# A decoder step in float32: inputs and outputs laid out by feature ahead of the launch, no turning of them on TensorE, products of ones while the first loads arrive

## The chip, the cores and the metric

The kernel runs on one core of a Trainium2 chip. The core has five engines that run beside each other: TensorE (PE in the rows; its weight loads are PEld), VectorE (DVE), ScalarE (ACT), GpSimd (POOL) and SyncE (SP), which here issues transfers. SBUF is the memory the engines work on, with 128 partitions; PSUM is what TensorE adds into; DRAM is reached by 16 DMA engines. The metric is device time in microseconds (us), lower is better. Before: 2800.08 us, median of three runs (2798.88 to 2800.47).

## The reference

One layer of a hybrid recurrent decoder for 272 prompt tokens (16 meta tokens, then 256) and eight sequences of eight sample tokens, together 336 columns; D = 2048, the feed-forward width is 5632.

```python
def layer(h, st, p, lead):
    s5_re, s5_im, C0, n0, m0, buf = st
    h = h + 0.5 * swiglu(rmsnorm(h, p['ffn1_norm']), p['ffn1_w_gate'], p['ffn1_w_up'], p['ffn1_w_down'])
    u = rmsnorm(h, p['mix_norm'])
    z = u @ p['w_in']
    y_s5, ns_re, ns_im = s5_mixer(z[..., :o0], ...)      # complex diagonal state space, GELU, gated linear unit
    y_ml, nC, nn_, nm, nbuf = mlstm_mixer(z[..., o0:o1], ...)   # causal convolution, matrix memory C, four heads
    gates = jax.nn.sigmoid(z[..., o5:])
    merged = gates[..., :D_MODEL] * (y_s5 @ p['w_branch_s5']) + gates[..., D_MODEL:] * (y_ml @ p['w_branch_mlstm'])
    h = h + merged @ p['w_out']
    h = h + 0.5 * swiglu(rmsnorm(h, p['ffn2_norm']), p['ffn2_w_gate'], p['ffn2_w_up'], p['ffn2_w_down'])
    return h, (ns_re, ns_im, nC, nn_, nm, nbuf)
# in a chunk of the mLSTM: num gets inter * einsum('nhvk,nlhk->nlhv', C0, q),
# and C = decay * C0 + einsum('nhs,nshv,nshk->nhvk', w_end, v, k)
```

After the layer the outputs are y = rmsnorm(h, final_norm) for the 256 + 64 = 320 live tokens, and the new states of S5, the mLSTM and the convolution.

## The kernel before

Activations lie by feature: a tile has 128 features on the partitions and the tokens as columns, 16 tiles for D. A large product takes a weight tile of 128 by 128 as the stationary operand and 336 columns (320 once the meta tokens are no longer needed) as the moving one. Every float32 number is split into two float32r parts, so a weight tile makes three products (`product`, L388 to L390: high by high, high by low, low by high).

`Weights` holds the order in which TensorE takes the weights. A load is 1 MB, a ring of three buffers (`wraw`) takes them from SyncE's queue, a load is issued when both halves of the load three before it have been split. A load has two halves of 24 products (four k tiles, two column tiles, three products each). `take` hands a half out and first emits the split of the half two ahead: ScalarE casts the high part (L95, tile `whi`), VectorE subtracts it (L96, `wlo`). All engines take their instructions in the order written; that order comes from the Python code, where generators (`tick`) put the small work of the mixers between the halves, one step a half, or two for those in `fast`.

At the start x lies in DRAM by token. `constants` loads it in three column pieces with halves of the first two weight loads between them; seven gain vectors come as rows over GpSimd's queue. `x_features` turns four tiles at a time on TensorE (L367 to L370, four pieces a tile), splits them (`norm_split`, L329 and L330) and copies them from PSUM to `h` (L377). The first pair of gate and up products (tile `sm`) runs between these groups: gate 0, turn, up 0, gate 1, turn, and so on, eight halves in all.

In the mixers TensorE also turns S5's parameters and states (L577, L583), S5's C matrices (L741), the convolution's old and new rows (L923, L924, L1117), the C state of the sample sequences before it is used (L1225, eight a value half, four heads by two value halves), the last S5 states (L1395) and the normaliser (L1294). A prompt's new memory is three products per value half (L1242).

In the last down product each finished pair of tiles is scaled by the final gain and turned back by token (`turned`, L1464), six turns a pair; `finish` sums squares over the partitions (L1477), takes the root (L1481), and ScalarE and VectorE scale the rows while the stores go out.

## Time and profile before

| what | us |
|---|---|
| three timed runs | 2800.47, 2800.08, 2798.88 |
| span of the profiled execution (first to last instruction) | 2797.4 |
| TensorE busy | 2776.8 |
| VectorE busy | 1600.3 |
| ScalarE busy | 1106.0 |
| GpSimd busy | 194.5 |

The profiled execution's own time is not given beside its span; the median of the timed runs is 2.7 us above it. Matmuls are pipelined and one's end is modelled, so a row's duration of 0.31 us holds the overlap with the next; the distance from start to start is what one costs. The DMA engines moved 459.03 MB, 164 GB/s over the span.

### The profile page before, as it was taken

The page shows a single profiled execution, that of the slowest core. Times are in us where ns is not written, and L with a number is a line of the kernel's source. Part 1 is how long each engine was busy: PE and PEld are TensorE (multiplying, and loading weights), DVE is VectorE, ACT ScalarE, POOL GpSimd, SP SyncE. Part 2 cuts the span into 40 slices and gives each one's busy share as a digit, 9 for nine tenths or more (in the row PEclk, how much of TensorE's full clock was granted, in tenths as well). Part 3 has the DMA queues.
Part 4 walks back from the last instruction along what each step waited for, and adds up shares of the span by engine and source line. Part 5 has one row for each costly group of instructions (what it writes and reads, how often), then busy time and mean ns, then how long its engine had stood idle before and what let it go on. Part 6 is the DMA issues. An engine that isn't in the chain of part 4 may idle for free.

```text
span 2797.4 us, 44767 instructions
## 1 busy us (share of the span) xinstructions
PE 2776.8 (99%) x18640; PEld 2759.9 (99%) x18640; DVE 1600.3 (57%) x2485; ACT 1106.0 (40%) x1617; POOL 194.5 (7%) x298
## 2 busy tenths in 40 slices
PE   9999999999999999999999999999999999999998
PEld 8999999999999999999999999999999999999998
DVE  6666565555544575767655556445445555445455
ACT  5433444444432353434344444443333333333334
POOL 4000001000000042000010100100000000000001
PEclk9999999999999999999999999999999999999999
DMA  6445544554444457566655666544444444454542
GB/s 183 148 137 179 156 160 159 186 166 158 157 165 141 140 178 197 188 197 203 205 166 170 204 200 206 172 148 151 151 152 150 151 151 147 142 164 137 165 146 88
DMA packets 375884, 459.03 MB, mean 164 GB/s; under 512 B 16338, under 2 KB 319422, under 8 KB 374641
## 3 DMA queue, kind: packets, MB, share of 16 engines
q1 hardware_dynamic: 360880, 417.33, 46.8%
q0 software_dynamic: 10336, 32.74, 3.4%
q10 hardware_dynamic: 4464, 6.09, 0.6%
q8 instruction: 147, 2.41, 0.4%
q14 instruction: 57, 0.46, 0.0%
HBM read 419.54 MB, written 36.57 MB: 163 GB/s over the span
## 4 chain that ended last, share of the span: by engine, by line
PE 97%; DVE 1%; ACT 1%; DMA 1%; issue 0%; SPq 0%; ACTq 0%; DVEq 0%
PE mm L388 30%; PE mm L390 30%; PE mm L389 30%; PE sm L388 1%; PE sm L390 1%; PE sm L389 1%; PE sm L1339 1%; PE sm L1232 0%; DVE slotB L330 0%; DVE wlo L96 0%; DMA aux<-u_dr 0%; PE sm L1384 0%; PE sm L765 0%; PE sm L1385 0%; PE sm L1225 0%
## 5 line engine op out<-in xcount | busy, mean ns | idle before, releaser
L96 DVE TENSOR_TENSOR wlo<-wraw,whi 128x1024 fp32r<-128x1024 f32 x727 | 881.9, 1225 | 653.5 <-ACT whi L95 652.8
L95 ACT CAST whi<-wraw 128x1024 fp32r<-128x1024 f32 x727 | 748.7, 1047 | 799.3 <-PE mm L389 774.3
L388 PE MATMUL mm<-slotA,whi 128*128 128x336 f32 (+1 forms) x2688 | 851.2, 317 | 0.3 <-DVE slotE L457 0.3
L390 PE MATMUL mm<-slotA,wlo 128*128 128x336 f32 (+1 forms) x2688 | 844.2, 314 | 0.0
L389 PE MATMUL mm<-slotB,whi 128*128 128x336 f32 (+1 forms) x2496 | 783.9, 314 | 0.0
L389 PE MATMUL mm<-quarter,whi 128*128 128x320 f32 (+1 forms) x1792 | 558.9, 312 | 0.0
L388 PEld LDWEIGHTS mm<-slotA,whi 128*128 128x128 f32 x2688 | 505.6, 188 | 2.8 <-issue 1.2
L390 PEld LDWEIGHTS mm<-slotA,wlo 128*128 128x128 f32 x2688 | 504.8, 188 | 0.2 <-DVE wlo L96 0.2
L388 PE MATMUL mm<-quarter,whi 128*128 128x320 f32 (+1 forms) x1536 | 481.2, 313 | 0.6 <-DVE slotE L457 0.6
L390 PE MATMUL mm<-quarter,wlo 128*128 128x320 f32 (+1 forms) x1536 | 480.4, 313 | 0.4 <-DVE wlo L96 0.4
L389 PEld LDWEIGHTS mm<-slotB,whi 128*128 128x128 f32 x2496 | 469.7, 188 | 1.2
L388 PE MATMUL mm<-slotB,whi 128*128 128x320 f32 x1472 | 455.1, 309 | 0.0
L390 PE MATMUL mm<-slotB,wlo 128*128 128x320 f32 x1472 | 454.8, 309 | 0.0
L389 PE MATMUL mm<-slotD,whi 128*128 128x320 f32 x1344 | 415.3, 309 | 0.0
L389 PEld LDWEIGHTS mm<-quarter,whi 128*128 128x128 f32 x1792 | 336.8, 188 | 0.0
L388 PEld LDWEIGHTS mm<-quarter,whi 128*128 128x128 f32 x1536 | 288.7, 188 | 1.1 <-issue 1.1
L390 PEld LDWEIGHTS mm<-quarter,wlo 128*128 128x128 f32 x1536 | 288.3, 188 | 0.8 <-DVE wlo L96 0.8
L388 PEld LDWEIGHTS mm<-slotB,whi 128*128 128x128 f32 x1472 | 276.3, 188 | 0.1
L390 PEld LDWEIGHTS mm<-slotB,wlo 128*128 128x128 f32 x1472 | 276.3, 188 | 0.0
L457 DVE SCALAR_TENSOR_TENSOR slotE<-mm,slotE 128x336 f32<-128x336 f32 (+1 forms) x352 | 171.4, 497 | 157.6 <-PE mm L390 148.7
L389 PEld LDWEIGHTS mm<-slotD,whi 128*128 128x128 f32 x1344 | 252.3, 188 | 0.1
L339 POOL TENSOR_TENSOR acc<-acc,sq 128x336 f32<-128x336 f32 (+1 forms) x58 | 61.1, 1054 | 1408.1 <-ACT sq L338 1406.1
(393 smaller groups left out, 1744.3 us busy)
## 6 DMA issues: line engine op xcount, KB each, us to landing
wraw<-in_ffn_w_down_dram SPq DMA_DIRECT2D x88, 1024.0 KB, 5.1
wraw<-in_ffn_w_gate_dram SPq DMA_DIRECT2D x87, 1024.0 KB, 5.1
wraw<-in_ffn_w_up_dram SPq DMA_DIRECT2D x87, 1024.0 KB, 5.1
wraw<-in_w_in_dram SPq DMA_DIRECT2D x64, 1024.0 KB, 5.7
wraw<-in_w_out_dram SPq DMA_DIRECT2D x16, 1024.0 KB, 5.5
w_dr<-slotD POOLq DMA_DIRECT2D x8, 1280.0 KB, 8.0
wraw<-in_w_branch_mlstm_dram SPq DMA_DIRECT2D x8, 1024.0 KB, 5.7
wraw<-in_w_branch_s_dram SPq DMA_DIRECT2D x8, 1024.0 KB, 5.5
```

What stands on the lines that cost most here:

```text
L95: k.nc.scalar.copy(hi, src)
L96: k.nc.vector.tensor_tensor(lo, src, hi.bitcast(F32), op=ALU.subtract)
L339: nc.gpsimd.tensor_tensor(self.acc[:, 0:n], self.acc[:, 0:n], sq, op=ALU.add)
L388: nc.tensor.matmul(ps[m], hi[:, k, c], a, start=first and k == 0, stop=False)
L389: nc.tensor.matmul(ps[m], hi[:, k, c], b, start=False, stop=False)
L390: nc.tensor.matmul(ps[m], lo[:, k, c], a, start=False, stop=last and k == 3)
L457: nc.vector.scalar_tensor_tensor(hm, ps[m], 0.5, hm, op0=ALU.mult, op1=ALU.add)
L1339: pe.matmul(ps[:, NSL * t:NSL * t + NSL], w1[:, a, t], u4[g % 2][:, t], start=True, stop=True)
```

## The change

A function outside the kernel (`lay_out`) writes the inputs in the layout that the tiles have: x by feature, with meta, prompt and sample tokens in one array; all vectors as columns of one array; the C state with the key on the partitions; every 1 MB weight load as one contiguous block of 128 rows of 8 KB. `lay_back` does the same for the outputs. No arithmetic is moved there except a repeated log_dt. In the kernel the turns of these are gone, each group of small loads is one load. The C state and its update keep the key on the partitions, so in the update v is now masked and split in place of k. The output is scaled by feature: the reciprocal root of the mean square is spread over partitions by three products, and 16 tiles are scaled, five on GpSimd, eleven on VectorE. At the start TensorE multiplies ones (`rouse`).

```diff
     def constants(self):
-        nc.scalar.dma_start(gain1, i["ffn1_norm"][0].rearrange("(a p) -> a p", p=P))
-        nc.scalar.dma_start(self.xs[2][64:80], meta)
-        for c, (lo, hi) in enumerate(((0, 512), (512, 1024), (1024, 2048))):
-            s = slice(lo, hi)
-            nc.sync.dma_start(self.xs[0][:, s], xp[0:128, s])
-            nc.sync.dma_start(self.xs[1][:, s], xp[128:256, s])
-            nc.sync.dma_start(self.xs[2][0:64, s], sm[:, s])
-            if c < 2:
-                self.w.load_half(0, c)
-                self.w.load_half(1, c)
+        xpart = lambda q, lo, hi: q.dma_start(e[:, NT * lo:NT * hi], i["x"][:, NT * lo:NT * hi])
+        nc.scalar.dma_start(cols[:, 0:120], i["vec"])
+        part(0, 0, 2)
+        xpart(nc.scalar, 0, 2)
+        xpart(nc.sync, 2, 4)
+        part(0, 2, 4)
+        part(1, 0, 4)
+        xpart(nc.sync, 4, 8)
+        part(0, 4, 8)
+        part(1, 4, 8)
+        xpart(nc.sync, 8, 12)
+        xpart(nc.sync, 12, 16)
...
+    def rouse(self):
+        pe = self.nc.tensor
+        o = self.ones
+        ps = self.mm_psum()
+        for _ in range(4):
+            pe.matmul(ps[:, 0:P], o, o, start=True, stop=True)
+        tiles = [self.mm_psum() for _ in range(3)]
+        for _ in range(5):
+            for t in (0, 1):
+                for m in (0, 1):
+                    pe.matmul(tiles[t][64 * m:64 * m + 64, 0:96], o[64 * t:64 * t + 64, 64 * m:64 * m + 64], o[64 * t:64 * t + 64, 0:96], start=True, stop=True)
+        for _ in range(4):
+            pe.matmul(tiles[2][:, 0:P], o, o, start=True, stop=True)
...
     def ffn(self, which):
-                        turned = self.x_features(0)
                         for part in range(2):
-                            next(turned)
                             self.w.first(part)
-                        next(turned, None)
+                            for m in (2 * part, 2 * part + 1):
+                                self.norm_split(m, h[:, m])
...
                             if which == 1 and ps is pg and j < 3:
-                                for _ in self.x_features(j + 1):
-                                    pass
+                                for m in range(4 * j + 4, 4 * j + 8):
+                                    self.norm_split(m, h[:, m])
...
     def mlstm(self):
-                for b in range(2):
-                    ps = self.sm_psum()
-                    for n in range(4):
-                        pe.transpose(ps[:, P * n:P * n + P], c0[b][:, n], self.ident)
-                    s.copy(c0t[b], ps)
-                yield from rest(2)
...
-                        pe.matmul(num[:, 256 + 8 * n:264 + 8 * n], c0t[n // 4][:, P * (n % 4):P * (n % 4) + P],
+                        pe.matmul(num[:, 256 + 8 * n:264 + 8 * n], c0[n // 4][:, n % 4],
...
-                up = self.sm_psum()
-                for t, n in enumerate((128, 112, 32)):
-                    pe.matmul(up[:, 0:P], vv(t, n), kw[0:n, t], start=t == 0, stop=t == 2)
+                if x == 0:
+                    up = self.sm_psum()
+                    for t, n in enumerate((128, 112, 32)):
+                        pe.matmul(up[:, 0:256], kw[0:n, t], self.vt[h][0:n, t], start=t == 0, stop=t == 2)
...
     def finish(self):
+        rb = self.sm_psum()
+        for t, (at, w) in enumerate(self.ENDS):
+            nc.tensor.matmul(rb[:, at:at + w], r[0:w, t:t + 1].to_broadcast([w, P]), self.ident[0:w, 0:w], start=True, stop=True)
+        rs = self.rstd_tile[:, 0:n]
+        nc.scalar.copy(rs, rb[:, 0:n])
...
+        for m in range(self.AIDED):
+            nc.gpsimd.tensor_tensor(self.h[:, m], self.h[:, m], rs, op=ALU.mult)
+            if m in (0, 2, 4):
+                store(nc.scalar, max(m - 1, 0), m + 1)
+        for m in range(self.AIDED, 16):
+            g = self.vec["final"][:, m:m + 1]
+            nc.vector.scalar_tensor_tensor(self.h[:, m], self.h[:, m], g, rb[:, 0:n], op0=ALU.mult, op1=ALU.mult)
+            if m == self.AIDED or (m - self.AIDED) % 2 == 0:
+                store(nc.sync, m if m == self.AIDED else m - 1, m + 1)
```

Three places show how the instructions move. SyncE's queue at the start, before (x by token in pieces, `slotD` and `aux`; weights by half):

```order
L238 DMA slotD<-in_x_prompt_dram 128x512
L239 DMA slotD<-in_x_prompt_dram 128x512
L240 DMA aux<-in_x_sample_dram 64x512
L76 DMA wraw<-in_ffn_w_gate_dram 128x4x256
L76 DMA wraw<-in_ffn_w_up_dram 128x4x256
...
L238 DMA slotD<-in_x_prompt_dram 128x1024
L239 DMA slotD<-in_x_prompt_dram 128x1024
L240 DMA aux<-in_x_sample_dram 64x1024
L67 DMA wraw<-in_ffn_w_gate_dram 128x8x256
```

The same queue after; `in_x_dram` and `in_weights_dram` are the new arrays, and the first two tiles of x go over ScalarE's queue:

```order
L127 DMA wraw<-in_weights_dram 128x512
L224 DMA slotE<-in_x_dram 128x672
L127 DMA wraw<-in_weights_dram 128x512
L127 DMA wraw<-in_weights_dram 128x1024
L224 DMA slotE<-in_x_dram 128x1344
L127 DMA wraw<-in_weights_dram 128x1024 x2
L224 DMA slotE<-in_x_dram 128x1344 x2
L119 DMA wraw<-in_weights_dram 128x2048 x143
```

The third weight load (L67 before, the first L119 after) stands behind all of x in both.

TensorE's first instructions, before: the gain (`sm<-ident,aux`), then pieces of x turned into `mm`, then the first half's products:

```order
L260 MATMUL sm<-ident,aux 128x16
L367 MATMUL mm<-ident,slotD 128x128
L368 MATMUL mm<-ident,slotD 128x128
L369 MATMUL mm<-ident,aux 128x64
L370 MATMUL mm<-ident,aux 128x16
...
L388 MATMUL sm<-slotA,whi 128x336
L389 MATMUL sm<-slotB,whi 128x336
L390 MATMUL sm<-slotA,wlo 128x336
```

and after, where ones stand in their place:

```order
L263 MATMUL mm<-ones 128x128 x4
L268 MATMUL mm<-ones 64x96 x20
L270 MATMUL mm<-ones 128x128 x4
L358 MATMUL sm<-slotA,whi 128x336
L359 MATMUL sm<-slotB,whi 128x336
L360 MATMUL sm<-slotA,wlo 128x336
```

Between the halves of this first pair the groups L367 to L370 of before have no counterpart.

TensorE in one value half of a head of the mLSTM, before (`slotE` holds the C state, loaded and turned; `quarter` is v; "..." are halves of the large products):

```order
L1225 MATMUL sm<-ident,slotE 128x128 x8
...
L1302 MATMUL sm<-aux,quarter_11167 128x256
L1303 MATMUL sm<-aux,quarter_11167 128x144
L1232 MATMUL sm<-slotE 128x8 x8
L1305 MATMUL sm<-aux,quarter_11167 128x96
...
L1242 MATMUL sm<-slotE,quarter_11167 128x128 x3
...
L1256 MATMUL sm<-km,vs 128x512
```

and after:

```order
L1204 MATMUL sm<-aux,quarter_10957 128x256
L1205 MATMUL sm<-aux,quarter_10957 128x144
L1143 MATMUL sm<-slotE 128x8 x8
L1207 MATMUL sm<-aux,quarter_10957 128x96
...
L1154 MATMUL sm<-quarter_10957,slotE 128x256 x3
...
L1162 MATMUL sm<-vm,ks 128x512
```

The eight turns are gone, L1154 stands only in a head's first value half, and L1162 has its operands swapped.

## Rows read from the trace of the kernel before

**Rows 1.** The page's first part: busy us, share of the span, instructions

```profile
PE 2776.8 (99%) x18640; PEld 2759.9 (99%) x18640; DVE 1600.3 (57%) x2485; ACT 1106.0 (40%) x1617; POOL 194.5 (7%) x298
```

**Rows 2.** Busy time by stretches, PE, PEld, DVE, ACT, POOL, PEclk, DMA share, GB/s

```profile
1030.00:1580.00 550.00, 549.95 (x3786) 541.23 (x3786) 358.85 (x659) 239.76 (x400) 71.05 (x121) 1.00 0.60 190
```

**Rows 3.** Order of time, the start: start us, us, engine, line, operation, [idle before]

```profile
4.99 0.18 PEld L367 LDWEIGHTS mm<-ident,slotD 128*128 128x128 f32 x1 [0.54 <-DMA slotD<-in_x_prompt_dram]
...
11.75 0.65 PE L388 MATMUL sm<-slotA,whi 128*128 128x336 f32 x1
...
16.12 0.48 PE L388 MATMUL sm<-slotA,whi 128*128 128x336 f32 x1
...
16.40 0.36 PE L389 MATMUL sm<-slotB,whi 128*128 128x336 f32 x1
...
41.59 0.32 PE L389 MATMUL sm<-slotB,whi 128*128 128x336 f32 x1
...
52.54 0.32 PE L388 MATMUL mm<-slotA,whi 128*128 128x336 f32 x1
```

**Rows 4.** Order of time, TensorE in the last down product

```profile
2759.58 0.82 PE L1464 MATMUL sm<-ident,hg 128*128 128x128 f32 x6
...
2761.62 0.30 PE L389 MATMUL mm<-quarter,whi 128*128 128x320 f32 x1
...
2769.16 0.82 PE L1464 MATMUL sm<-ident,hg 128*128 128x128 f32 x6
...
2769.97 0.30 PE L389 MATMUL mm<-quarter,whi 128*128 128x320 f32 x1
...
2773.34 0.82 PE L1464 MATMUL sm<-ident,hg 128*128 128x128 f32 x6
```

**Rows 5.** Order of time, TensorE at a turn of the C state

```profile
1318.28 0.60 PE L1225 MATMUL sm<-ident,slotE 128*128 128x128 f32 x4
1318.72 0.60 PE L1225 MATMUL sm<-ident,aux 128*128 128x128 f32 x4
...
1319.31 0.31 PE L389 MATMUL mm<-slotB,whi 128*128 128x320 f32 x1
```

**Rows 6.** Order of time, TensorE at a prompt's new memory

```profile
1328.89 1.02 PE L1242 MATMUL sm<-slotE,quarter 128*128 128x128 f32 x6
...
1330.10 0.31 PE L389 MATMUL mm<-slotB,whi 128*128 128x320 f32 x1
```

**Rows 7.** Busy time by stretches, start and tail, columns as in rows 2

```profile
0.00:22.40 22.40, 15.74 (x69) 12.41 (x70) 10.84 (x26) 9.98 (x16) 4.32 (x13) 1.00 0.96 262
...
16.40:17.60 1.20, 1.20 (x9) 1.20 (x9) 1.16 (x2) 0.00 (x0) 0.00 (x0) 1.00 1.03 410
...
2788.00:2789.00 1.00, 0.00 (x0) 0.00 (x0) 0.75 (x1) 0.58 (x2) 0.00 (x0) 0.55 1.03 380
...
2795.00:2796.00 1.00, 0.00 (x0) 0.00 (x0) 0.00 (x0) 0.00 (x0) 0.00 (x0) 0.50 0.50 156
```

**Rows 8.** Order of time, ScalarE and VectorE in the first pair

```profile
21.11 1.04 ACT L95 CAST whi<-wraw 128x1024 fp32r<-128x1024 f32 x1
...
25.39 1.45 DVE L96 TENSOR_TENSOR wlo<-wraw,whi 128x1024 fp32r<-128x1024 f32 x1 [0.41 <-ACT whi L95]
```

**Rows 9.** Order of time, TensorE in the tail

```profile
2781.55 0.31 PE L390 MATMUL mm<-quarter,wlo 128*128 128x320 f32 x1
...
2784.50 1.40 PE L1477 MATMUL sm<-ones,sq 128*128 128x1 f32 x12
```

**Rows 10.** The page's part 5, by line: count, busy us, mean ns, idle before

```profile
L457 DVE SCALAR_TENSOR_TENSOR slotE<-mm,slotE 128x336 f32<-128x336 f32 (+1 forms) x352 | 171.4, 497 | 157.6 <-PE mm L390 148.7
L339 POOL TENSOR_TENSOR acc<-acc,sq 128x336 f32<-128x336 f32 (+1 forms) x58 | 61.1, 1054 | 1408.1 <-ACT sq L338 1406.1
```

**Rows 11.** DMA issues: count, KB each, median us from issue to landing

```profile
wraw<-in_ffn_w_gate_dram SPq DMA_DIRECT2D x87, 1024.0 KB, 5.1
...
slotD<-w_dr SPq DMA_DIRECT2D x8, 768.0 KB, 6.8
```

More of the change, by code (lines that the diff above doesn't have):

```diff
@@ L44, with weight_order, add, both @@
 AHEAD = 2
+def weight_order():
+    chunks, seq = [], []
+    def add(name, r0, r1, c0, c1):
+        chunks.append((name, r0, r1, c0, c1, (r1 - r0) // P))
+        return len(chunks) - 1
+    def both(*cs):
+        for c in cs:
+            seq.extend([(c, 0), (c, 1)])
+    def deep(name, col, rows=D):
+        both(*(add(name, a, a + 1024, col, col + 256) for a in range(0, rows, 1024)))
+    def ffn(n):
+        wg, wu, wd = (f"ffn{n}_w_{x}" for x in ("gate", "up", "down"))
+        def down(b):
+            both(*(add(wd, 512 * b, 512 * b + 512, 512 * q, 512 * q + 512) for q in range(4)))
+        for b in range(NBLK):
+            for pr in range(2):
+                col = 512 * b + 256 * pr
+                if b == 0 and pr == 0:
+                    for a in range(0, D, 1024):
+                        g, u = (add(w, a, a + 1024, col, col + 256) for w in (wg, wu))
+                        seq.extend([(g, 0), (u, 0), (g, 1), (u, 1)])
+                else:
+                    deep(wg, col)
+                    deep(wu, col)
+                if pr == 0 and b:
+                    down(b - 1)
+        down(NBLK - 1)
+    ffn(1)
+    for cols in ((0, 4096), (GATES + D, GATES + 2 * D), (GATES, GATES + D)):
+        for col in range(*cols, 256):
+            deep("w_in", col)
+    for name, cols in (("w_branch_mlstm", D), ("s5_w_glu", 1024), ("w_branch_s5", D)):
+        for col in range(0, cols, 256):
+            deep(name, col, 1024)
+    for col in range(0, D, 256):
+        deep("w_out", col)
+    ffn(2)
+    return chunks, seq
 class Weights:
@@ L53, in __init__ @@
         self.chunks = chunks
+        self.src = k.ins["weights"]
         self.seq = seq
@@ L533, in ffn_done @@
                 self.final_piece(m)
-        if which == 2:
-            self.post(1, lambda: self.turned(q))
-        else:
+        if which == 1:
             m = slice(2 * q, 2 * q + 2)
@@ L721, in s5_weights @@
             tg = slice(4 * g, 4 * g + 4)
[L722 to L728 removed]
+            nc.gpsimd.dma_start(bc, i["s5_bc"][g])
             for t in range(4):
@@ L1139, in mlstm @@
         n4 = lambda t: t.rearrange("p (n k) -> p n k", n=4)
-        ring = [n4(e[:, 2688:3200]), n4(e[:, 3200:3712]), n4(take(512))]
-        c0t = [e[:, 3712 + 512 * j:4224 + 512 * j] for j in range(2)]
+        ring = [n4(e[:, 2688 + 512 * j:3200 + 512 * j]) for j in range(3)]
+        vs = [e[:, 4224:4480], e[:, 4480:4736]]
         kw = e[:, 4736:5120].rearrange("p (t k) -> p t k", t=3)
-        ks = [e[:, 5120:5248], take(P)]
         qi, qn = e[:, 5248:5312], e[:, 5312:5376]
@@ L1158, in load @@
                 h, x, b = pieces[loaded[0]]
-                nc.sync.dma_start(ring[loaded[0] % 3], cin[4 * b:4 * b + 4, h, P * x:P * x + P, :].rearrange("n v k -> v n k"))
+                nc.sync.dma_start(ring[loaded[0] % 3], cin[h, x, b])
                 loaded[0] += 1
@@ L1475, in finish @@
         for j, a in enumerate((self.acc, *sq)):
-            for t, (at, _) in enumerate(self.ENDS):
-                nc.tensor.matmul(ps[:, t:t + 1], a[:, at:at + P], self.ones[:, 0:1], start=j + t == 0, stop=j + t == 4)
+            for t, (at, w) in enumerate(self.ENDS):
+                nc.tensor.matmul(ps[0:w, t:t + 1], a[:, at:at + w], self.ones[:, 0:1], start=j + t == 0, stop=j + t == 4, skip_group_check=True)
             if j == 0:
@@ L1530 @@
     r = _run(nc, [arrays], core_ids=[0])
-    return tuple(r.results[0][f"out_{j}_dram"] for j in range(len(_OUTS)))
+    return lay_back({n: _np.asarray(r.results[0][f"out_{n}_dram"]).reshape(shape) for n, shape in _OUTS.items()})
```

392 lines of the change are left out of this document (129 added, 263 removed).

## The prediction

> **What bounds the kernel now.** I read the page's first part, then the busy time by stretches, then the order of time at both ends. TensorE is busy 2776.8 of 2797.4 us [rows 1]. The reader is to see where the missing 20.6 us lie: in the mixers' stretch 1030 to 1580 it is busy 549.95 of 550.00 us, with VectorE at 358.85 and ScalarE at 239.76 [rows 2], so nearly all idle time lies in the first 12 and the last 15 us. As busy can hide waiting, I then looked at the distance between starts: products of 336 columns stand 0.154 us apart (71 of them from 41.59 to 52.54) [rows 3], those of 320 columns 0.146 us (23 from 2769.97 to 2773.34) [rows 4]. These distances are back to back, so away from the ends every instruction taken off TensorE shortens the run by the distance it opens, as long as nothing else becomes late. At the ends, transfers and the other engines decide. The span is 2797.4 us; the median of the three runs is 2800.08, so 2.7 us lie around the span. I work on the span and add them.
>
> **The middle: work taken off TensorE.** The price of a turn by TensorE is read from a place where eight stand in a row. The eight turns of the C state begin at 1318.28, and the second product after them starts at 1319.31 [rows 5]; without them it would start one distance of 0.146 after 1318.28. So eight cost 0.88 us, one 0.11. C is turned at eight places (four heads, two value halves): 8 x 0.88 = 7.0 us. The remaining turns between the ends are 16 for S5's C matrices, 8 for the new convolution rows, 9 in conv_setup, 7 in s5_parameters, 6 for the last S5 states, one each for the gains and the normaliser: 48 x 0.11 = 5.3 us. The turns of v, of k, of S5's B and of the gating rows stay.
>
> The new memory of a prompt is now one product per head with 256 moving columns, in place of two with 128. One such group costs 1330.10 - 1328.89 - 0.146 = 1.06 us [rows 6], eight of them 8.5. The moved columns are the same in total, the instructions half. If columns set the price nothing is saved, if instructions do, half, 4.2 us; I take 1.8, somewhat below the middle, as the three unequal row counts of a group cost the same once per group either way. The products of the new sample states keep their count and columns with swapped operands: nothing. The sum of the middle is 7.0 + 5.3 + 1.8 = 14.1, between 12.3 and 16.5 us.
>
> ScalarE and VectorE lose the copies that followed these turns and two table loads are added on ScalarE. Neither is late in this stretch [rows 2], so I count nothing; the cover is the 191 us that VectorE is idle there. Where the turned copy of C is gone, the state products read the loaded ring itself. The reload of a ring slot is issued after the same update, four steps of the large products (two halves, 7 us) ahead of its use, before and after, and against it stand one store and one load. If this cover were gone, TensorE would wait in order, and behind it the next products.
>
> **The start.** Before, the first product starts at 11.75; until 16.40 products stand 0.28 us apart, then 0.154 [rows 3]. 336 columns in 0.28 us are 1.2 GHz, in half of that 2.4, although the window's clock column reads 1.00 throughout [rows 7]: of that clock the distances are the better witness here. Between the halves x is turned, four tiles at a time. The eight halves of this first pair end at 52.54.
>
> After, the first 256 KB of weights land at about 5.0, as the first 256 KB of x did [rows 3]; x0 and x1, 344 KB on ScalarE's queue beside it, about 6; then a split of x on ScalarE and VectorE, so the first product at about 7.0. Eight halves of 24 products at 0.154 are 29.6 us, so without any wait the pair ends at 36.6: 15.9 us saved. That is the one end. But x (2.75 MB), two weight loads (2.1 MB) and the third (1.05 MB) now stand on one queue in this order, 5.96 MB with the gains, and TensorE needs the third load after four halves, at 7.0 + 14.8 = 21.8, while whi and wlo of it and the split of x8 must be made before. By the window's mean, 262 GB/s up to 22.4 [rows 7], the bytes are moved at 22.7; a transfer's bytes are done some 1.5 us before it is known to have landed (at the end of the span the last bytes move before 2796 and the span ends at 2797.40 [rows 7]), so 24.2. Without the seven small gain loads and the 64-row loads I expect 335 GB/s from 2.3 us on (an estimate: the first issue at 0.8, bytes some 1.5 us behind it), between the mean and the best stretch, 410 [rows 7]: 20.1 + 1.5 = 21.6. I take 22.5, in between. From there ScalarE's cast takes 1.04 and VectorE's second part 1.45 beside a busy POOL [rows 8], then VectorE splits x8: 3.0 us, 0.3 us for x9 to x11 at 0.5 us each, then four halves, 14.8: the pair ends at 22.5 + 18.1 = 40.6, and 52.5 - 40.6 = 11.9 us are saved. With 262 GB/s counted from 2.3 us only, the third load lands at 26.5, the pair ends at 44.6: 7.9 us, the other end.
>
> So the work on ones is worth little by itself. It fills TensorE from the moment the ones are written and lets the first two halves run at 0.154 instead of 0.28 for the 17 products that now stand slow, 2.1 us, but these two stand ahead of the wait for the third load, and what they gain is waited for there. Should the 28 products of ones (two instructions each, the twenty small ones perhaps side by side) run until 11 us, the four halves ahead of that wait are late by 4, and the pair ends at 42: inside the range given.
>
> The Trainium skill, DMA: Bandwidth & Descriptors, Specifications, gives about 358 GB/s as what the memory gives one core; by it 5.96 MB from 2.3 us on are moved at 18.9 at the earliest, landed at 20.4, and the pair would end no sooner than 38.5, 14.0 us saved. The trace shows 410 GB/s for 1.2 us, above that, but 262 over the whole stretch; the measurement decides, so the end without a wait keeps a chance.
>
> **The end.** Before, turning the output takes from 2759.58 to 2761.62 less one product, 1.9 us, as two groups wait there for their operand, and 2769.97 - 2769.16 - 0.146 = 0.66 us at each of four further places [rows 4]: 4.5 us, all in the row of products, and gone. The tail, from the last product's start at 2781.55 to 2797.40, is 15.85 us [rows 9]. After, with T for that start: the last addition ends at T + 0.9, its square at 1.4, the sums over partitions at 2.2, two roots and the reciprocal at 3.0, the three products that spread it at 3.9. Then VectorE makes eleven tiles of 0.50 us from PSUM, to T + 9.3, and POOL five of 1.05 us behind a copy of 0.5, to T + 9.7 [rows 10]; their last stores need about 0.4 to issue and 2.6 to land, and all 2.6 MB at 380 GB/s [rows 7] from T + 5.5 are moved at T + 12.4, landed at 13.9. POOL beside VectorE may take 1.3 a tile. I take T + 14.3: 1.5 saved, between 3 saved and 1 lost.
>
> **Sum.** 14.1 + 11.9 + 4.5 + 1.5 = 32.0 us; 2797.4 - 32.0 = 2765.4, with the 2.7 around the span 2768.1. I predict 2768. With the ends of start, middle and tail together the forecast runs from 2800.1 - 39.9 = 2760 to 2800.1 - 23.7 = 2776.
>
> **Rivals.** First, the start waits for nothing: the loads run at the best rate and the clock is up. For it speaks the 410 GB/s stretch, against it the mean. It saves 15.9 there: 2764. Second, the loads stay at the slow rate and TensorE's waits are long enough to drop its clock again: at the end of before the last sums stop at 2785.9 [rows 9] and the clock column reads 0.55 in 2788 to 2789 [rows 7], so a wait of less than 3 us suffices. Then the start saves 7.9 less 2.1: 2774. Third, the middle's 14.1 us are given back, since VectorE's chain in the heads or the reload of a C slot becomes late when the products between get fewer. Against it speak 191 us of idle VectorE. If three quarters come back: 2768 + 10.6 = 2779. Fourth, slower: the weight loads of 1 MB, now one contiguous block with 8 KB per partition, could be slower than rows of 1 KB. TensorE takes 1 MB in two halves, 48 x 0.146 = 7.0 us, and there are 364 loads; from 7.1 us a load the whole saving is gone. The loads of contiguous 6 KB rows do take 6.8 us for 768 KB, which scaled to 1 MB is 9.1: 364 x 2.1 us later, about 3530. Against it: these were queued behind weights on the same queue, and a weight load of 1 KB rows lands in 5.1 [rows 11].
>
> **How the numbers follow.** My forecast has 0.60, the first rival 0.13, the second 0.15, the third 0.09, the slower one 0.03. Differences below 0.2% (5.6 us) could not be told from none here. All but the last lie more than that below 2800.08: faster 0.96, same 0.01, slower 0.03. The range reaches from just below the fast start to the middle given back: 2758 to 2779.
>
> **What would show it.** Right: in the changed profile the first product starts near 7 at 0.154 apart, the ninth half waits for the cast of the third load until about 24 to 26, the first pair ends near 40.6, no turns stand between products at the heads, and the last product starts about 30.5 us earlier. Wrong: a pair that ends at 37 or 45 (the load rate), waits of TensorE at the state products (third rival), weight loads that land later than 7 us (fourth), or a tail longer than 16 us.

## The result, and the profile after

The changed kernel takes 2770.93 us (median of 4 runs, 2770.21 to 2771.51), against 2799.48 of the kernel before in the same session: ratio 0.9901, 95% interval 0.9887 to 0.9915. The forecast was 2768, with a range of 2758 to 2779. The profiled execution took 2770.21 us, its span 2768.5, which is 28.9 less than before.

Lines have new numbers: the three products of a large one are L358, L359, L360; the casts and second parts of the weights L146 and L147; the split of x L323 and L324; the squares L332 and L333; the sum of a norm L344.

First the page's busy line and the stretches, columns as in [rows 1] and [rows 2]:

```profile
PE 2749.8 (99%) x18453; PEld 2736.3 (99%) x18453; DVE 1581.2 (57%) x2433; ACT 1079.0 (39%) x1520; POOL 155.9 (6%) x234
```

```profile
5.00:10.00 5.00, 4.20 (x22) 3.67 (x21) 3.11 (x6) 3.65 (x7) 0.00 (x0) 1.00 1.03 401
10.00:15.00 5.00, 5.00 (x35) 5.00 (x34) 3.13 (x5) 3.19 (x6) 0.00 (x0) 1.00 1.03 419
15.00:20.00 5.00, 5.00 (x34) 5.00 (x34) 2.58 (x5) 2.70 (x6) 2.92 (x3) 1.00 1.01 418
1010.00:1560.00 550.00, 546.14 (x3718) 536.15 (x3717) 361.75 (x650) 230.18 (x362) 61.56 (x108) 1.00 0.54 192
```

The loads of the start now run at 401 to 419 GB/s in these stretches. Over the first 22.4 us the mean is 351, where it was 262 before [rows 7]. And the mixers' stretch, in which TensorE was busy for all but 0.05 us [rows 2], now has 3.9 us without work. What TensorE waits for (us in total, times, longest; L1098 turns k of a head):

```profile
PE sm L1098 <- ACT aux L1094: 1.4, 1, 1.4
PE mm L358 <- ACT whi L146: 1.4, 1, 1.4
...
PE mm L344 <- POOL acc L333: 0.7, 1, 0.7
...
PE mm L360 <- DVE wlo L147: 0.7, 1, 0.7
```

None of these four stands in the kernel before at that size. In order of time, TensorE at the start, in the heads and at the end:

```profile
3.13 1.88 PE L268 MATMUL mm<-ones 64*64 64x96 f32 x40
4.94 2.05 PE L270 MATMUL mm<-ones 128*128 128x128 f32 x8
7.60 0.42 PE L358 MATMUL sm<-slotA,whi 128*128 128x336 f32 x1 [0.61 <-ACT slotA L323]
8.20 0.42 PE L359 MATMUL sm<-slotB,whi 128*128 128x336 f32 x1 [0.19 <-DVE slotB L324]
...
23.00 0.31 PE L358 MATMUL sm<-slotA,whi 128*128 128x336 f32 x1
23.46 0.42 PE L359 MATMUL sm<-slotB,whi 128*128 128x336 f32 x1
...
38.76 0.32 PE L358 MATMUL mm<-slotA,whi 128*128 128x336 f32 x1
...
43.34 0.83 PE L344 MATMUL mm<-acc,ones 128*128 128x336 f32 x2 [0.72 <-POOL acc L333]
...
1287.90 0.55 PE L1098 MATMUL sm<-ident,slotE 128*128 128x128 f32 x3 [1.44 <-ACT aux L1094]
...
1385.21 0.41 PE L358 MATMUL mm<-slotA,whi 128*128 128x320 f32 x1 [1.42 <-ACT whi L146]
...
1386.47 0.42 PE L360 MATMUL mm<-slotA,wlo 128*128 128x320 f32 x1 [0.70 <-DVE wlo L147]
...
2753.72 0.31 PE L360 MATMUL mm<-quarter,wlo 128*128 128x320 f32 x1
```

The ones end at 6.99 (4.94 + 2.05) and the first product starts at 7.60 in place of 11.75. The first pair ends at 38.76 in place of 52.54 [rows 3], the last product starts at 2753.72 in place of 2781.55 [rows 9]. Matching the 17472 large products of the two traces one by one gives where the 28.9 us came from:

| part | forecast | measured | how |
|---|---|---|---|
| start, to the end of the first pair | 11.9 | 13.8 | 52.54 - 38.76 |
| the first norm's sum | 0 | -1.0 | TensorE's distance over it 0.47 before, 1.45 now |
| middle | 14.1 | 10.5 | lead of the changed kernel 12.8 us behind that sum, 23.3 behind the mixers |
| turns of the output | 4.5 | 4.5 | lead 27.8 at the last product |
| tail | 1.5 | 1.1 | 15.85 before, 2768.5 - 2753.72 now |
| sum | 32.0 | 28.9 | |

### The profile page after: what moved, and what is told of

It is laid out like the page before. It is cut to its first block, busy times and chain, and to the rows that moved or that the text cites. A ratio compares the mean times of both kernels' runs of the same rounds, so it can differ in the third digit from the quotient of the medians.

```text
span 2768.5 us, 44091 instructions
## 1 busy us (share of the span) xinstructions
PE 2749.8 (99%) x18453; PEld 2736.3 (99%) x18453; DVE 1581.2 (57%) x2433; ACT 1079.0 (39%) x1520; POOL 155.9 (6%) x234
## 4 chain that ended last, share of the span: by engine, by line
PE 96%; DVE 1%; ACT 1%; DMA 1%; issue 0%; POOL 0%; ACTq 0%; DVEq 0%; SPq 0%; POOLq 0%
PE mm L358 30%; PE mm L360 30%; PE mm L359 30%; PE sm L1143 0%; DMA wraw<-in_weights_dram 0%; ACT whi L146 0%; DVE slotB L324 0%; PE sm L1241 0%; POOL acc L333 0%; PE sm L359 0%; PE sm L358 0%; PE sm L360 0%; DVE wlo L147 0%; PE sm L1287 0%; PE sm L698 0%
## 5 line engine op out<-in xcount | busy, mean ns | idle before, releaser
L147 DVE TENSOR_TENSOR wlo<-wraw,whi 128x1024 fp32r<-128x1024 f32 x727 | 882.0, 1224 | 649.1 <-ACT whi L146 648.9
L146 ACT CAST whi<-wraw 128x1024 fp32r<-128x1024 f32 x727 | 748.8, 1047 | 879.9 <-PE mm L359 838.9
L358 PE MATMUL mm<-slotA,whi 128*128 128x336 f32 (+1 forms) x2688 | 849.4, 316 | 1.7 <-ACT whi L146 1.4
L360 PE MATMUL mm<-slotA,wlo 128*128 128x336 f32 (+1 forms) x2688 | 844.4, 314 | 0.7 <-DVE wlo L147 0.7
L359 PE MATMUL mm<-slotB,whi 128*128 128x336 f32 (+1 forms) x2496 | 784.0, 314 | 0.0
L359 PE MATMUL mm<-quarter,whi 128*128 128x320 f32 (+1 forms) x1792 | 558.9, 312 | 0.0
L358 PEld LDWEIGHTS mm<-slotA,whi 128*128 128x128 f32 x2688 | 505.6, 188 | 4.7 <-issue 2.5
L360 PEld LDWEIGHTS mm<-slotA,wlo 128*128 128x128 f32 x2688 | 504.8, 188 | 1.1 <-DVE wlo L147 1.1
L358 PE MATMUL mm<-quarter,whi 128*128 128x320 f32 (+1 forms) x1536 | 480.8, 313 | 0.6 <-DVE slotE L427 0.6
L360 PE MATMUL mm<-quarter,wlo 128*128 128x320 f32 (+1 forms) x1536 | 480.3, 313 | 0.0
L359 PEld LDWEIGHTS mm<-slotB,whi 128*128 128x128 f32 x2496 | 469.7, 188 | 1.2
L358 PE MATMUL mm<-slotB,whi 128*128 128x320 f32 x1472 | 455.1, 309 | 0.0
L360 PE MATMUL mm<-slotB,wlo 128*128 128x320 f32 x1472 | 454.8, 309 | 0.0
L359 PE MATMUL mm<-slotD,whi 128*128 128x320 f32 x1344 | 415.3, 309 | 0.0
L359 PEld LDWEIGHTS mm<-quarter,whi 128*128 128x128 f32 x1792 | 336.8, 188 | 0.0
L358 PEld LDWEIGHTS mm<-quarter,whi 128*128 128x128 f32 x1536 | 288.7, 188 | 1.1 <-issue 1.1
L360 PEld LDWEIGHTS mm<-quarter,wlo 128*128 128x128 f32 x1536 | 288.3, 188 | 0.0
L358 PEld LDWEIGHTS mm<-slotB,whi 128*128 128x128 f32 x1472 | 276.3, 188 | 0.1
L360 PEld LDWEIGHTS mm<-slotB,wlo 128*128 128x128 f32 x1472 | 276.3, 188 | 0.0
L359 PEld LDWEIGHTS mm<-slotD,whi 128*128 128x128 f32 x1344 | 252.3, 188 | 0.1
L333 POOL TENSOR_TENSOR acc<-acc,sq 128x336 f32<-128x336 f32 (+1 forms) x58 | 61.7, 1064 | 1476.7 <-ACT sq L332 1474.7
```

The source lines that it names most:

```text
L146: k.nc.scalar.copy(hi, src)
L147: k.nc.vector.tensor_tensor(lo, src, hi.bitcast(F32), op=ALU.subtract)
L333: nc.gpsimd.tensor_tensor(self.acc[:, 0:n], self.acc[:, 0:n], sq, op=ALU.add)
L358: nc.tensor.matmul(ps[m], hi[:, k, c], a, start=first and k == 0, stop=False)
L359: nc.tensor.matmul(ps[m], hi[:, k, c], b, start=False, stop=False)
L360: nc.tensor.matmul(ps[m], lo[:, k, c], a, start=False, stop=last and k == 3)
```

## The experiments

Each kernel is the changed one but for the edit shown, or builds on another run where the text says so. A span, like the two columns behind it, is that of one profiled execution; the same program's executions scatter, so small differences between two spans say nothing by themselves. The session's median of before was 2797.7 to 2798.5.

| run | median us (range) | ratio to before (95%) | span | first product | first pair's end |
|---|---|---|---|---|---|
| changed | 2770.93 (2770.21 to 2771.51) | 0.9901 (0.9887 to 0.9915) | 2768.5 | 7.60 | 38.76 |
| e1 | 2770.99 (2770.72 to 2771.18) | 0.9902 (0.9887 to 0.9917) | 2769.3 | 7.58 | 39.01 |
| e2 | 2771.76 (2771.30 to 2772.90) | 0.9906 (0.9891 to 0.9920) | 2770.2 | 6.32 | 38.77 |
| e3 | 2766.38 (2766.12 to 2766.62) | 0.9886 (0.9871 to 0.9900) | 2764.4 | 7.57 | 39.31 |
| e5 | 2770.98 (2770.48 to 2772.19) | 0.9902 (0.9885 to 0.9918) | 2770.4 | 7.61 | 39.08 |
| e6 | 2770.30 (2769.51 to 2771.13) | 0.9902 (0.9887 to 0.9916) | 2767.8 | 6.45 | 38.12 |
| e7 | 2771.42 (2770.45 to 2772.20) | 0.9905 (0.9888 to 0.9921) | 2770.2 | 6.67 | 38.43 |
| e9 | 2765.67 (2765.47 to 2766.04) | 0.9885 (0.9871 to 0.9900) | 2764.1 | 6.56 | 39.24 |
| e10 | 2765.08 (2764.84 to 2765.70) | 0.9881 (0.9864 to 0.9897) | 2763.6 | 6.67 | 38.27 |
| e11 | 2765.26 (2764.97 to 2765.57) | 0.9881 (0.9867 to 0.9896) | 2763.9 | 6.92 | 38.63 |
| e12 | 2765.19 (2764.59 to 2765.46) | 0.9881 (0.9866 to 0.9896) | 2762.9 | 6.52 | 38.20 |
| e13 | 2765.26 (2764.87 to 2765.53) | 0.9881 (0.9865 to 0.9898) | 2763.8 | 6.54 | 39.23 |
| e14 | 2773.41 (2772.90 to 2774.00) | 0.9909 (0.9893 to 0.9926) | 2772.3 | 7.75 | 38.99 |

### The heads: e3, e5, e14

e3 puts the steps of a head back where they were (the step between the copies of k and of v goes, two empty steps come ahead of each value half):

```diff
-                yield
                 vn, vr = self.vt[h][i, 2], vs[b].bitcast(F32R)
...
+                yield from rest(2)
                 num = self.sm_psum()
```

> The changed kernel with the heads' steps where the kernel before had them: two empty steps ahead of the products of each value half again, and the copies of v in the same step as those of k, so 31 steps a head in place of 29. Theory A (the heads shifted against the gates' sigmoids, and in two places ScalarE's work of both falls together): TensorE's waits in the heads, 1.4 us at the turns of k and 2.1 at one half's casts, go below 0.5 in sum, and the span is 3.0 to 3.6 us shorter than 2768.5. Theory B (with fewer products between, ScalarE and VectorE have less cover wherever the steps stand): at least 2 us of such waits remain, at these or other places, and the span is within 1 us.

e5 leaves the sigmoid out:

```diff
-        nc.scalar.activation(g, t, AF.Sigmoid)
+        nc.scalar.activation(g, t, AF.Identity)
```

> The changed kernel with the sigmoid of the gating rows left out (the rows are stored as they are), which takes 8 table loads of 1.28 us off ScalarE, and those back to the exponential and the root beside them. Theory A (the table loads between sigmoid, exponential and root make ScalarE late in the heads): 16 table loads fewer or nearly so, the waits of 1.4 and 2.1 us at the heads vanish, span 3 to 3.6 us shorter than 2768.5. Theory B (ScalarE is late because it stands in order behind a gating row whose product is not done, table or not): at least half of the waits stays.

In e3 the waits are gone: 549.64 busy us in the stretch that had 546.14, and the heads take 4.1 us less (the lead over the changed kernel grows from 0.4 to 4.5), more than the 3.0 to 3.6 of theory A, which stands. In the run's own session e3 lies 4.6 us under e1 and e5, which keep the waits.

```profile
1010.00:1560.00 550.00, 549.64 (x3746) 540.14 (x3745) 362.42 (x651) 231.44 (x364) 61.65 (x108) 1.00 0.56 194
```

In e5 all three waits are there, to the tenth, though the eight table loads of the sigmoid are gone. So it is the order that matters, as theory B had it. (e5's span is 1.9 us longer than the changed kernel's, its median the same: some 1.5 us of it are products at half the rate behind these waits, see the last section.) ScalarE in the changed kernel, at the wait of 1.42:

```profile
1380.06 0.47 ACT L928 ACTIVATE gs<-gt 128x320 f32<-128x320 f32 x1 [2.93 <-DVE gt L927]
...
1380.92 1.28 ACT L1092 ACT_TABLE_LOAD   x1 [0.39 <-ACT gs L928]
1382.21 1.08 ACT L1092 ACTIVATE aux<-aux 128x256 f32<-128x256 f32 x3
...
1383.36 0.86 ACT L1105 ACTIVATE slotE<-sm,aux 128x128 f32<-128x128 f32 x3
1384.11 1.05 ACT L146 CAST whi<-wraw 128x1024 fp32r<-128x1024 f32 x1
```

ScalarE is idle for 2.93 us ahead of a gating row that VectorE has not handed over; everything behind it stands. VectorE:

```profile
1378.41 1.21 DVE L147 TENSOR_TENSOR wlo<-wraw,whi 128x1024 fp32r<-128x1024 f32 x1
1379.55 0.48 DVE L927 TENSOR_TENSOR gt<-mm,rstd 128x320 f32<-128x320 f32 x1
```

VectorE has no idle time from 1374.91 until its step for this row (L927) at 1379.55, so at this place it is not the row's product that is late, as the expectation had it, but VectorE, which has other work ahead of that step. On ScalarE then come the store, a table load, a head's exponentials and its scaling of k, and only then the cast that TensorE waits for. In e3, same place:

```profile
1379.99 0.47 ACT L928 ACTIVATE gs<-gt 128x320 f32<-128x320 f32 x1 [1.69 <-DVE gt L927]
1380.37 1.04 ACT L146 CAST whi<-wraw 128x1024 fp32r<-128x1024 f32 x1
1381.43 1.28 ACT L1092 ACT_TABLE_LOAD   x1
1382.72 1.08 ACT L1092 ACTIVATE aux<-aux 128x256 f32<-128x256 f32 x3
```

The cast stands right behind the gating row, ahead of the exponentials. And in e5 the row without its sigmoid starts at the same time:

```profile
1380.09 0.47 ACT L928 ACTIVATE gs<-gt 128x320 f32<-128x320 f32 x1 [4.23 <-DVE gt L927]
...
1384.14 1.05 ACT L146 CAST whi<-wraw 128x1024 fp32r<-128x1024 f32 x1
```

The 1.28 us that the table load took are now idle time (4.23 in place of 2.93), and the cast comes at 1384.14 in place of 1384.11. The Trainium skill, PSUM — Partial Sum Buffer, Engine vs sequencer instructions, calls ScalarE's queue strictly first in, first out; these rows agree. The other wait on ScalarE, 1.44 us at 1287.90, stands behind a gating row too: ScalarE was idle 1.69 us for it, then came a table load and the exponentials that TensorE waited for.

e14 takes e3 and puts the eight turns of C back, without their copies:

```diff
+                for b in range(2):
+                    ps = self.sm_psum()
+                    for n in range(4):
+                        pe.transpose(ps[:, P * n:P * n + P], c0[b][:, n], self.ident)
                 yield from rest(2)
```

> The kernel with the heads' steps as before (span 2764.4, none of the waits in the heads), and the eight turns of the C state on TensorE put back at each of the eight places, where they stood, without the copies that read them; nothing uses their result. The prediction priced the eight at 0.88 us a place, 7.0 in all; the distances of the two traces give 0.79 to 0.80, 6.4. Theory A (each instruction on TensorE costs its distance, nothing is hidden): span 2770.4 to 2771.6. Theory B (part of it falls into time in which TensorE waits anyway, so the turns were worth less than the distances say): below 2769.5.

The span is 7.9 us longer than e3's, at 2772.3 above theory A's 2770.4 to 2771.6. The heads make 7.2 of it, 0.90 a place; the rest is at the start and the first norm's sum, where the two executions differ. One place:

```profile
1300.86 0.31 PE L360 MATMUL mm<-slotA,wlo 128*128 128x320 f32 x1
1301.01 1.04 PE L1141 MATMUL sm<-ident,slotE 128*128 128x128 f32 x8
1301.80 0.39 PE L358 MATMUL mm<-slotA,whi 128*128 128x320 f32 x1
1302.03 0.30 PE L359 MATMUL mm<-slotB,whi 128*128 128x320 f32 x1
1302.17 0.31 PE L360 MATMUL mm<-slotA,wlo 128*128 128x320 f32 x1
```

From 1300.86 to 1302.17 there are 1.31 us in place of 3 x 0.147: 0.87 more. The expectation's 0.79 was read over the one distance of 0.94; the distance behind it, 0.23, also grows. Theory A: the full price is paid, and the prediction's 0.88 was the right one.

### The start: e1, e2, e6, e7

e1 leaves the products of ones out:

```diff
-        self.rouse()
```

> The changed kernel without the 28 products of ones. Theory A (the ones bring TensorE to its full rate before the first real product): the first product still starts near 7.6 us, about 17 to 23 products then stand 0.28 us apart instead of 0.154, and the end of the first pair (38.75 us with the ones) moves to 40.3 to 41.0; span 1.5 to 2.3 us longer than 2768.5. Theory B (the step of the prediction: what the ones gain is waited for at the third weight load): the slow products are there, but the fifth half still starts at 23.0 +- 0.3 and the span changes by less than 0.5 us. Theory C (the rate is up without them): distances of 0.154 from the first product, span the same.

The rate is as A said (if for fewer products: eight distances of 0.28 from 8.63 to 10.87), the gain nearer to B:

```profile
7.58 0.65 PE L357 MATMUL sm<-slotA,whi 128*128 128x336 f32 x1 [7.58 <-ACT slotA L322]
...
10.31 0.48 PE L359 MATMUL sm<-slotA,wlo 128*128 128x336 f32 x1
10.59 0.48 PE L357 MATMUL sm<-slotA,whi 128*128 128x336 f32 x1
...
39.01 0.32 PE L357 MATMUL mm<-slotA,whi 128*128 128x336 f32 x1
```

The fifth half starts at 24.19, 1.2 us later, and B's 23.0 was a miss. But the waits of 0.3 us at the fifth and of 0.3 at the seventh half are gone, the pair ends 0.25 later, and behind it the wait of 1.0 at the norm's sum goes as well. The medians are the same.

The 0.25 us is no measure of the ones: e3, e5 and e14 have the changed kernel's start, ones included, and end the pair at 39.31, 39.08 and 38.99 against 38.76. In e3 the ones doubled their rate part of the way (0.213 us apart, then 0.111), ended at 6.09 in place of 6.99, and TensorE waited longer for x:

```profile
4.93 1.16 PE L270 MATMUL mm<-ones 128*128 128x128 f32 x8
7.57 0.42 PE L358 MATMUL sm<-slotA,whi 128*128 128x336 f32 x1 [1.48 <-ACT slotA L323]
...
9.00:10.00 1.00, 1.00 (x6) 1.00 (x5) 1.00 (x3) 1.00 (x2) 0.00 (x0) 0.50 1.03 423
```

Eleven distances of 0.28 followed; in e5, behind a wait of 1.82, nine. So in two of four executions the ones did not give the first products their full rate.

e2 lays every weight load out in rows of 1 KB (2 KB for the down weights, whose tiles are 512 columns wide):

```diff
+        return self.src[c].rearrange("a b -> (a b)").rearrange("(k p c) -> p k c", k=self.chunks[c][5], p=P)
...
-        self.k.nc.sync.dma_start(self._tile(c), self.src[c])
+        self._tile(c)
+        self.k.nc.sync.dma_start(self.raw[c], self._rows(c))
```

> The changed kernel with each weight load lying in DRAM as rows of 1 KB (by k tile, then partition) in place of 8 KB per partition; the same bytes on the same queue in the same order. Theory A (the size of the rows sets the rate of the start): between 5 and 20 us 260 to 330 GB/s instead of 401 to 419, the third load lands at 24 to 26 us instead of 20.5, the fifth half waits 2 to 4 us for its cast, and the span is 2 to 4 us longer than 2768.5. Theory B (the kernel before was slow there through its many small loads and the loads of x by token, not through the rows of the weights): the third load lands at 20.5 +- 0.7 and the span is within 0.7 us. Both: a load later in the program lands in about 5.1 us in place of 4.8, and nothing waits for it, as TensorE takes 7 us for one.

Neither theory holds as written. Columns as above:

```profile
5.00:10.00 5.00, 4.81 (x31) 4.55 (x30) 3.90 (x7) 3.46 (x6) 0.00 (x0) 1.00 1.06 376
10.00:15.00 5.00, 5.00 (x34) 5.00 (x34) 3.04 (x6) 3.71 (x6) 0.00 (x0) 1.00 1.08 391
15.00:20.00 5.00, 5.00 (x34) 5.00 (x33) 1.66 (x3) 1.77 (x5) 3.25 (x3) 1.00 1.07 350
```

The longer rows give 7 to 19% more in these stretches. From 0 to 22.4 us the means are 351 in the changed kernel and 329 GB/s in e2, so rows of 1 KB for the weights alone do not make the 262 of before. The first pieces came a microsecond earlier in e2, so the third load's cast started at the same time (20.65 against 20.61) and the pair ended at the same time.

e6 and e7 ask why they came earlier. They change the first load alone, to contiguous pieces with rows of 1 KB (e6, shown), and of 2 KB (e7, with j=4):

```diff
+        if c == 0:
...
+            src = self.src[0].rearrange("a b -> (a b)").rearrange("(j p c) -> p j c", j=8, p=P)[:, s]
```

> The changed kernel with the first weight load alone lying in DRAM as rows of 1 KB, all others as 8 KB per partition. With all loads in rows of 1 KB the first 256 KB were cast at 4.12 us in place of 5.03 and the first product started at 6.32 in place of 7.60, but the third load came later (the fifth half at 22.22 behind waits of 1.2 us). Theory A (the form of the first load sets the first, that of the later ones the rate behind it): the cast at about 4.1, the first product at 6.3 +- 0.3, 390 to 420 GB/s from 5 to 20 us, no wait over 0.6 us at the fifth half, the first pair ends at 37.4 to 38.0 in place of 38.76. Theory B (what comes first is limited by the bytes in flight, and 1 KB rows in all loads made the difference): the cast near 5.0, the first product near 7.5.

> The changed kernel with the first weight load alone lying in DRAM as four blocks, each contiguous, with a row of 2 KB per partition: rows as long as those that the first issue reads in the changed kernel (256 of 1024 KB of 8 KB partitions), but without the stride of 8 KB between them. Theory A (the length of the rows decides): as in the changed kernel, first cast at 5.0, first product at 7.5 +- 0.3. Theory B (the stride between the rows decides): as with rows of 1 KB, first cast at 4.1, first product at 6.3 +- 0.3.

The first cast starts at 5.03 in the changed kernel (first row), at 3.92 in e6 and at 3.75 in e7 (second row):

```profile
5.03 0.62 ACT L160 CAST whi<-wraw 128x512 fp32r<-128x512 f32 x1 [2.01 <-DMA wraw<-in_weights_dram]
...
3.75 0.62 ACT L165 CAST whi<-wraw 128x512 fp32r<-128x512 f32 x1 [0.74 <-DMA wraw<-in_weights_dram]
```

So a first load read at a stride of 8 KB comes later than one in contiguous blocks, at the same row length of 2 KB; why, no run here shows. On this A of e6 and B of e7 stand. The product starts 1.2 and 0.9 us earlier, the pair ends only 0.6 and 0.3 earlier, about the size of the scatter seen above; e6's A had it at 37.4 to 38.0. The rate was A's other miss: 381 GB/s from 5 to 20 us in e6, not 390 to 420. What came earlier was not more: over the first 8 us the three kernels moved 230, 235 and 240 GB/s.

### What waits behind the front: e9 to e13

e9 joins e3, e6 and the norm's sum a half later:

```diff
-                    self.post(2, lambda: self.norm_end(self.mm_psum))
+                    self.post(3, lambda: self.norm_end(self.mm_psum))
```

> The changed kernel with three edits: the heads' steps as in the kernel before, the first weight load in rows of 1 KB, and the sum over partitions of the first norm (with the gating behind it) one half later. If what the runs before showed adds up, against 2768.5 of the changed kernel: 4.1 us less at the heads, 0.9 less at the first norm, 0.8 to 1.4 less at the start, so a span of 2762.0 to 2762.8, against 2764.4 with the steps alone. If the wait at the first norm only moves (VectorE's gating behind it becomes late, or the PSUM tiles of the pair are held longer), 2763 to 2764.

The sum's wait is gone (TensorE's distance over it is 0.48), but the span of 2764.1 is only 0.3 shorter than that of e3, whose first products ran slow: the first product stands a microsecond earlier than there, and the pair ends at the same time, through new waits at the second and fifth halves. The expected sum, 2762.0 to 2762.8, was a miss.

e10 adds the third load ahead of the last quarter of x; e11 is e10 without ones:

```diff
+        self.w.load_one()
         xpart(nc.sync, 12, 16)
```

> As the kernel with the three edits (steps, first load in rows of 1 KB, first norm's sum a half later), and the third weight load issued ahead of the last quarter of x (688 KB) instead of behind it. The first pair ended at 38.1 to 39.3 in every kernel so far, whether its first product started at 6.3 or 7.6 and whether it ran at 0.154 or 0.28 at first. Theory A (the bytes ahead of the third load set that end): 688 KB at 415 GB/s are 1.7 us, the fifth half starts at 21.2 to 21.6 without a wait of more than 0.3, the pair ends at 36.8 to 37.8 in place of 39.24, and the span is 2762.0 to 2763.2 in place of 2764.1. Theory B (the split of x on ScalarE and VectorE behind the cast sets it): fifth half at 22.5 or later, the pair's end within 0.5 of 39.2.

> The same kernel (third weight load ahead of the last quarter of x) without the products of ones. In the changed kernel leaving them out cost 0.25 us at the first pair's end. Theory A (what the ones gain is waited for at the third load, and only there): with that load early the slow first products, 12 to 17 at 0.28, now cost 1.5 to 2.1 us at the first pair's end against the run with ones. Theory B (the ones are worth nothing whatever the loads): below 0.5 us.

The cast of the third load starts at 19.04 and the fifth half has no wait, but the pair ends at 38.27, since the wait is now at the seventh half:

```profile
30.84 0.42 PE L365 MATMUL sm<-slotB,whi 128*128 128x336 f32 x1 [0.79 <-DVE slotB L330]
```

Half of A was right (the fifth half), its end was not. Here too it is ScalarE's order: the squares of x wait for GpSimd, and behind them stand a cast and the split of x.

```profile
26.30 0.49 ACT L338 ACTIVATE sq<-slotE 128x336 f32<-128x336 f32 x1 [1.30 <-POOL acc L339]
27.28 0.49 ACT L338 ACTIVATE sq<-slotE 128x336 f32<-128x336 f32 x1 [0.50 <-POOL acc L339]
27.68 1.03 ACT L151 CAST whi<-wraw 128x1024 fp32r<-128x1024 f32 x1
```

e11's pair ends 0.36 later than e10's: B. e12 gives the squares places of their own, e13 is e12 without ones:

```diff
-            sq = self.tmp.tile([P, NT], F32, tag="t0", name="sq")[:, 0:n]
+            sq = self.tmp.tile([P, NT], F32, tag="t0", name="sq")[:, 0:n] if own is None else own
...
-                    sq = self.squares(h)
+                    sq = self.squares(h, own=(lambda m: self.slots["D"][:, NT * m:NT * m + NT]) if which == 1 else None)
```

> As the kernel with the third weight load ahead of the last quarter of x, and the squares of x for the first norm in places of their own (an unused slot) instead of two buffers in turn, so that ScalarE does not stand behind GpSimd's additions between two of them (1.3 and 0.5 us, seen ahead of the cast for the seventh half). Theory A (that stand sets the seventh half): the cast that stood at 27.68 comes at 26 or earlier, TensorE's wait of 0.8 us at the seventh half goes, the pair ends at 37.2 to 37.6 in place of 38.27, span 2762.6 to 2763.0 in place of 2763.6. Theory B (the loads set it): the wait stays at 0.5 or more.

> The same kernel without the products of ones. With every later wait of the first pair gone, the ones should be worth what they give at the front: the first 12 or so products 0.126 slower each and a start later by 0 to 0.3, so the pair ends 1.4 to 1.9 us later than with them (38.6 to 39.4). If the ones are still worth less than 0.5 us, something else waits behind the front.

The cast moves from 27.68 to 24.91 and the wait at the seventh half goes (A), but in this execution waits of 0.4 stand at the third half and elsewhere, and the pair ends at 38.20, not at the 37.2 to 37.6 expected. Without the ones it ends 1.0 us later (one execution each; 1.4 to 1.9 were expected), and the medians differ by 0.07 (2765.19 and 2765.26). The best kernels are these: 2765.1 to 2765.3, some 5.7 us below the changed one, of which e3's step order makes 4.5.

## Why the prediction was right, and where it was not

**Direction and size.** Right: 2770.9 against 2768, by the mechanism named: instructions taken off a TensorE that has no idle time shorten the run by their distances. That the sum came so near owes something to luck: the start gave 1.9 us more than forecast, the middle, the first norm's sum and the tail 5.0 less, and the 2.7 us added around the span set a median beside another execution's span; the profiled execution here has 1.7 (2770.21 and 2768.5). The turns of the output are 4.5 us as forecast, with one product every 0.146 us through the last down product.

**The middle, price.** Right. C's eight turns cost 0.88 in the forecast, 0.90 in e14. The memory of a prompt, read as in the prediction: 1.06 a place before at eight places, now 1.69 at four (the group starts at 1306.68, the second product behind it at 1308.52; 0.146 taken off), 1.7 saved where 1.8 were taken. The 48 other turns were not tried by themselves.

**The middle, cover: the step that failed.** "Neither is late in this stretch [rows 2], so I count nothing; the cover is the 191 us that VectorE is idle there." ScalarE was idle even longer (230 of 550 us busy), and still late at two places of 550 us. 3.6 us of waits came back (1.44, 1.42, 0.70). In e3, without them, the middle is 14.6 us in place of 10.5: the price of 14.1 held, and the cover put at nothing cost 4.1. VectorE's idle time was no cover either: at the place shown it had none for the 4.6 us ahead of the step that ScalarE stood for. An average of idle time says nothing of an engine that works in order: the change took two empty steps from each value half and added two to each head, so other work fell in front of a cast. The third rival named the place, but TensorE waited for ScalarE's chain, with VectorE only one link of it, and the share was a quarter, not three quarters.

**The start, size.** The saving of 11.9 was 13.8. The 4.0 us that the forecast let TensorE wait for the third load did not come: the load was sized at 22.5 and the fifth half put at 25.8, but its cast started at 20.61 and the half at 23.00, straight behind the fourth, with 0.3 us lost at its second product and 0.3 at the seventh half. (The prediction's sign speaks of the ninth half; the pair has eight, and by its own working the fifth is meant.) The rate was 401 to 419, not the 335 estimated: the stretch of 410 [rows 7] was the better row. The mean of 262 was not time without transfers: the share of the DMA engines is 0.96 over that stretch [rows 7], and here, before, it is full at 309 GB/s:

```profile
10.00:15.00 5.00, 5.00 (x19) 4.25 (x19) 4.27 (x9) 3.42 (x7) 0.00 (x0) 1.00 1.09 309
```

What slowed these transfers no run here isolates; SyncE issued the third load at 11.54 before, at 7.27 now. The first rival (no wait, 15.9) was nearer than the forecast on the loads, but the first product came at 7.60, not 7.0: the first two tiles of x landed at 6.9, not 6. The page that the forecast drew on, the Trainium skill, DMA: Bandwidth & Descriptors, Specifications, has 358 GB/s a core; the trace passes it by up to 61. Another page of the Trainium skill, HBM Reference, Specifications (TRN2), says that a core that streams alone measures about 425; the trace, with one core at work and 401 to 419, agrees.

**The ones.** "The work on ones is worth little by itself": right as far as the runs can tell. The medians with and without them differ by less than 0.2 us (e10 and e11, e12 and e13, the changed kernel and e1). The pair's end, 0.25, 0.4 and 1.0 us earlier with them, is one execution each, and with the same start and ones it lies anywhere from 38.76 to 39.31. The reason given, a wait for the third load, is not what the changed kernel shows, since its fifth half starts without one; e10 and e12 took the waits of the fifth and seventh halves away, and others came up.

**The first norm's sum** was no term. It costs 1.0 us: the pair ends 13.8 us earlier, GpSimd's last addition of squares only 10.6 (at 53.87 before, at 43.29 now).

**The tail.** 14.8 against 14.3: VectorE's eleven tiles start at T + 4.6, where T + 3.9 was forecast. They waited for ScalarE's copy from the same PSUM tile, which ended at 2758.30:

```profile
2757.87 0.43 ACT L1365 COPY rstd<-sm 128x320 f32<-128x320 f32 x1 [1.37 <-PE sm L1363]
2758.33 5.13 DVE L1375 SCALAR_TENSOR_TENSOR slotE<-slotE,vcols,sm 128x320 f32<-128x320 f32 x11 [1.62 <-ACT rstd L1365]
```

No run here tried the tail, so this is read from the trace alone.

**The slower rival** (contiguous 8 KB rows slower than 7.1 us a load) fell: the page has 4.8 us from issue to landing for 362 loads, 5.1 before [rows 11], and 5.5 in e2, where 5.1 was expected. What the layout of the weights is worth after the start e2 shows: it is 0.95 us behind the changed kernel at the last product, 0.7 of it from two waits near 1606 to 1610.

## What to carry to other kernels

Price what leaves a full engine by its distances (all of them, the one behind the group too), but check the cover instruction by instruction on each engine that works in order: which cast, copy or load for the full engine stands behind an instruction that waits for something else. When a change alters how many steps a helper takes, keep the old steps first and time that alone; here the order was worth a sixth of the whole gain. At a start that hands work on just in time an earlier first instruction is soon waited for: here it came 0.9 to 1.3 us earlier (e2, e6, e7) and the first pair ended 0.0 to 0.6 earlier. And two executions of one program can differ by more than an edit gives, so small edits need the medians of several.

## What the runs showed of the hardware

- A short wait brings TensorE's clock down, if not each time. In e3 the ones ended at 6.09 and TensorE waited 1.48 us for x; the clock column then reads 0.50 from 9 to 11 us and products of 336 columns stand at 0.28, 1.2 GHz. In e5 it waited 1.82 and the same followed. In the changed kernel the wait was 0.61, in e14 1.23, and the clock stayed at 1.00. In e1 products of 320 columns stood at 0.27 for some 3 us behind waits of 1.4 and 0.7 in the heads, with the clock column at 0.50 from 1387 to 1389; in the changed kernel, behind the same waits, at 0.146. Where it happens (e1, e5, e7) it costs some 1.5 us.
- The clock column can read 1.00 while TensorE runs at half the rate: in e1 from 8.63 to 10.87, with products of 336 columns 0.28 us apart.
- Products of 64 by 64 on four parts of the array run side by side: 40 of them with 96 columns take 1.88 us in the ones, where 8 of 128 by 128 with 128 columns take 2.07 right behind them (rows of the trace, two for each product).
- The same 256 KB at the start came 1.1 to 1.3 us earlier from contiguous blocks than at a stride of 8 KB (casts at 3.92 and 3.75 against 5.03; 5.06 to 5.12 in e1, e3, e5 and e14, which have the stride too).
